# Scaling the shared-key heads behind their values product, and interleaving the long input's first passes with the short projection

## The chip, the cores and the metric

The kernel runs on one core of one Trainium2 chip. A core has five engines with instruction queues of their own: TensorE (PE in the profile; its weight loads are listed as PEld), VectorE (DVE), ScalarE (ACT), GpSimd (POOL) and SyncE (SP), which here issues every DMA. Each queue is worked off in order; an instruction that waits holds up all that stand behind it on its engine. The metric is the device time of one execution in microseconds.

## The reference

The program is one layer of an encoder, applied with shared weights to a long input (1024 tokens) and a short one (512 tokens), each with 16 learned tokens in front. Model width is 1024.

```python
n = rms_norm(h, g_mix)
qa, ka, va, qb, kb, vb = split(n @ w_in)          # 18 blocks of 128 columns
# group A: 8 query heads of 64 columns, 2 key/value heads, each shared by 4 query heads
qa, ka = rope(rms_norm(qa)), rope(rms_norm(ka))
oa = softmax(qa @ ka.T / 8) @ va
# group B: 4 heads, each the difference of two softmax maps
qb, kb = rope(qb), rope(kb)
ob = (softmax(q0 @ k0.T / 8) - lam * softmax(q1 @ k1.T / 8)) @ vb
ob = rms_norm(ob, g_subln) * (1 - lam_init)
h = h + concat(oa, ob) @ w_out
n = rms_norm(h, g_ffn)
h = h + (gelu(conv3(n @ w_gate)) * (n @ w_up)) @ w_down
return rms_norm(h, g_final)[:, 16:]
```

All inputs and outputs are float32. The change touches the front of this: the norm of the input, the order of the projection `n @ w_in`, and the softmax of group A.

## The kernel before

**Products.** A float32 product is made of three fast ones: both operands are split into a rounded part (`hi`) and the rest (`lo`), and `mm3` (L121 to L123) adds hi·hi, hi·lo and lo·hi in PSUM. A split (`split`, L114 and L115) is a copy on ACT and a subtraction on DVE, or on POOL where the caller says so. `load_weight` loads a weight block of [128, 1024] and splits it; where `g.splits` is a list, it notes the two instructions there. `dense` is one output tile: 8 blocks of the contraction, 24 matmuls. Products with `ones_d`, `ones_hd`, `ones_v` (to sum squares over partitions) and the transposes are plain float32 matmuls, which the profile lists as two records each.

**Projection** (`projection`, once per input s; s = 0 is the long input with 1040 columns in chunks of 384, 384 and 272; s = 1 the short one with 528 in chunks of 256 and 272). Columns are tokens. First come eight passes, one per 128 rows of the input: load x, scale and round it on ACT (L234, `xhi`), subtract on DVE (L235, `xlo`), square on ACT (L238). The squares of the short input are summed at once by TensorE into two PSUM tiles (L241); those of the long input are added up on POOL (L245, `acc`), and three matmuls sum them over partitions at the end (L255). `rsqrt_newton` makes `rstd` from the sums, chunk by chunk. Then come 18 weight blocks: K and V of group A, then the four Q blocks of A alternating with the V blocks of B, then K and Q of B in turn. `qk_a` multiplies a product by `rstd` (L312), squares it, sums it (L318), norms and rotates it (`rotary`); `values` multiplies (L333) and transposes (L339). The blocks of B need no norm of their own, so their rope tables are multiplied by `rstd` beforehand on POOL (L366). Results go to DRAM (`g.qk`, `g.v`, `g.vt`).

**Attention** (`attention`). For group A, a block is 512 queries of one head: eight blocks for the short input, sixteen for the long one. For each 128 queries `softmax` makes the scores (L431, L432), DVE moves them out of PSUM with a running maximum (L433), ACT takes the exponential in place and sums it (L438, `l`), DVE takes 1/l (L442) and multiplies the whole tile of [128, keys] by it (L508). When four tiles stand, `weighted_v` transposes them on TensorE in pieces of 128 keys (L456), splits each piece (ACT and DVE), and multiplies by the values (L470, L471), queries along the columns. `finish_a` adds the two halves of the result (ACT L487, DVE L489) into `o_a`, which is stored to `g.oT`. Group B has its own scaling (L532) and is not touched.

**Order.** Each function is a generator that yields the matmul columns it has issued, and `merge` interleaves two of them by weights. The short projection is written alone, to its end. Then the short attention is merged with the long projection, then the long attention with the short input's output projection and feed-forward layer, then the rest of the long input follows. What is written is only the preference: a planner simulates the machine while it lays out the program and gives each engine the first instruction, in the order of writing, that it takes to be ready. `tc.issue_after` (`behind` here) ties an instruction behind another on the same engine's queue; it is an order, not a wait for its end. Before the change, ACT's and DVE's passes of the long input are tied behind the short input's norm (`g.norm_of_short`), and the long input's first product behind the short projection's fourteenth (`g.short_products`). All DMAs go through SP.

## Time and profile before

| | |
|---|---|
| Time before, median of 3 runs | 2134.44 us (2131.06 to 2139.33) |
| The profiled execution | 2127.9 us, of which the span shown by the trace is 2126.1 us |
| TensorE busy in the span | 2040.4 us (96%) |
| VectorE busy | 1725.0 us (81%) |
| ScalarE busy | 1156.0 us (54%) |
| GpSimd busy | 560.8 us (26%) |
| DMA | 296.31 MB, mean 139 GB/s |

The table's busy times are sums over stages with different limits. The lines of a group in the profile give: source line, engine, operation, tiles written and read, shape and count, then the busy time, the mean time of one in ns, and the idle time of that engine just before them with what ended it. A line of waits names the engine and line that waited, what it waited for, the total in us, how often, and the longest. A row of a stretch gives, for each engine, its busy time and number of instructions, then the granted share of TensorE's clock and the DMA share. The chain of waits goes back from the last instruction of a stretch to what released it, step by step; its shares tell which engine the time depended on.

### The profile page before, as it was taken

To read this page: it belongs to the slowest core of one execution; us is meant where nothing else is said; L and a number is where in the kernel's file an instruction comes from. 1 tells how busy PE (TensorE), PEld (TensorE's weight loads), DVE (VectorE), ACT (ScalarE), POOL (GpSimd) and SP (SyncE) were. 2 spreads that over 40 slices of the span, in tenths; PEclk is the share of its full clock that TensorE was granted. 3 is DMA by queue.
4 is the path that set the end of the run, shared out by engine and by line. 5 is a ranking of instruction groups with operands and counts; after the bars stand their busy time and mean duration, and the time that the engine had idled before them with its cause. 6 is when DMAs were issued, how large, how long until landed. Compare 5 with 4: busy or idle time off the path is not lost.

```text
span 2126.1 us, 35236 instructions
## 1 busy us (share of the span) xinstructions
PE 2040.4 (96%) x12302; PEld 1822.3 (86%) x12302; DVE 1725.0 (81%) x3786; ACT 1156.0 (54%) x2253; POOL 560.8 (26%) x494
## 2 busy tenths in 40 slices
PE   6999999998999999999999999988999999999998
PEld 6988888997887989999989999987887777778877
DVE  6878889767879788888998885578778878879886
ACT  6635566544567556666666765345444444435454
POOL 4653233453112000000000000421544444330112
PEclk9999999999999999999999999999999999999999
DMA  7563435457621322223352225996322232247443
GB/s 255 176 203 130 119 111 171 153 178 236 209 79 56 105 75 67 74 82 118 104 187 88 86 97 147 276 290 217 107 100 90 101 113 84 94 167 260 119 126 127
DMA packets 171426, 296.31 MB, mean 139 GB/s; under 512 B 21456, under 2 KB 90608, under 8 KB 170736
## 3 DMA queue, kind: packets, MB, share of 16 engines
q1 hardware_dynamic: 171248, 294.05, 42.5%
q8 instruction: 97, 1.59, 0.3%
q14 instruction: 81, 0.66, 0.1%
HBM read 211.13 MB, written 82.85 MB: 138 GB/s over the span
## 4 chain that ended last, share of the span: by engine, by line
PE 76%; DVE 12%; DMA 4%; issue 3%; ACT 2%; POOL 1%; SPq 0%; DVEq 0%; ACTq 0%; POOLq 0%
PE ps_mm L121 17%; PE ps_mm L123 17%; PE ps_mm L122 17%; PE ps_t L456 5%; PE ps_s L431 3%; PE ps_s L432 3%; PE ps_s L122 2%; PE ps_s L123 2%; PE ps_s L121 2%; DVE p L433 2%; PE ps_o L471 2%; DVE w_lo L115 1%; PE ps_o L470 1%; DVE acc L972 1%; DMA m<-oT 1%
## 5 line engine op out<-in xcount | busy, mean ns | idle before, releaser
L121 PE MATMUL ps_mm<-xhi,w_hi 128*128 128x258 f32 (+3 forms) x1264 | 383.1, 303 | 12.3 <-ACT xhi L114 5.6
L122 PE MATMUL ps_mm<-xlo,w_hi 128*128 128x258 f32 (+3 forms) x1264 | 378.4, 300 | 0.3 <-POOL xlo L115 0.3
L123 PE MATMUL ps_mm<-xhi,w_lo 128*128 128x258 f32 (+3 forms) x1264 | 377.1, 299 | 0.3 <-DVE w_lo L115 0.3
L433 DVE TENSOR_SCALAR_CACHE_REDUCE p<-ps_s 114x344 f32<-114x344 f32 (+4 forms) x562 | 257.8, 489 | 28.1 <-PE ps_s L432 16.8
L114 ACT CAST pt_hi<-ps_t 128x512 fp32r<-128x512 f32 (+6 forms) x360 | 169.6, 484 | 180.8 <-PE ps_t L456 153.3
L121 PEld LDWEIGHTS ps_mm<-xhi,w_hi 128*128 128x128 f32 x1264 | 239.6, 190 | 18.3 <-ACT xhi L114 7.8
L438 ACT ACTIVATE p<-p,nm 114x1040 f32<-114x1040 f32 (+5 forms) x212 | 214.8, 1013 | 70.5 <-DVE nm L436 69.3
L115 DVE TENSOR_TENSOR w_lo<-w_f,w_hi 128x1024 fp32r<-128x1024 f32 (+1 forms) x182 | 195.2, 1080 | 67.3 <-ACT w_hi L114 66.8
L122 PEld LDWEIGHTS ps_mm<-xlo,w_hi 128*128 128x128 f32 x1264 | 240.0, 190 | 1.9 <-POOL xlo L115 0.8
L123 PEld LDWEIGHTS ps_mm<-xhi,w_lo 128*128 128x128 f32 x1264 | 239.4, 190 | 1.2 <-DVE w_lo L115 0.5
L114 ACT CAST w_hi<-w_f 128x1024 fp32r<-128x1024 f32 (+1 forms) x199 | 167.4, 856 | 79.3 <-PE ps_mm L122 52.2
L115 DVE TENSOR_TENSOR pt_lo<-ps_t,pt_hi 128x512 fp32r<-128x512 f32 (+4 forms) x312 | 172.0, 562 | 42.5 <-ACT pt_hi L114 40.9
L115 POOL TENSOR_TENSOR a_lo<-gate,a_hi 128x256 fp32r<-128x256 f32 x44 | 43.1, 981 | 540.9 <-ACT a_hi L114 521.0
L431 PE MATMUL ps_s<-k,q 128*114 128x348 f32 (+4 forms) x552 | 182.7, 336 | 3.2 <-DVE p L433 3.0
L456 PE MATMUL ps_t<-ident,p 128*128 128x128 f32 (+7 forms) x1188 | 182.4, 269 | 0.9 <-DVE nm L436 0.5
L121 PE MATMUL ps_s<-xhi,w_hi 128*128 128x256 f32 (+4 forms) x480 | 148.2, 311 | 23.2 <-DVE t L333 7.7
L432 PE MATMUL ps_s<-k,q 128*114 128x348 f32 (+4 forms) x552 | 170.3, 313 | 0.0
L456 PEld LDWEIGHTS ps_t<-ident,p 128*128 128x128 f32 (+7 forms) x1188 | 139.9, 135 | 29.1 <-issue 6.8
L123 PE MATMUL ps_s<-xhi,w_lo 128*128 128x256 f32 (+4 forms) x480 | 147.0, 307 | 3.2 <-DMA w_lo<-wo 3.0
L122 PE MATMUL ps_s<-xlo,w_hi 128*128 128x256 f32 (+4 forms) x480 | 148.7, 311 | 1.2 <-DVE xlo L115 0.5
L122 PE MATMUL ps_mm<-t_lo,w_hi 128*128 128x512 f32 (+2 forms) x368 | 142.8, 388 | 1.4 <-DVE t_lo L115 1.4
L121 PE MATMUL ps_mm<-t_hi,w_hi 128*128 128x512 f32 (+2 forms) x368 | 142.8, 388 | 0.0
(273 smaller groups left out, 5269.7 us busy)
## 6 DMA issues: line engine op xcount, KB each, us to landing
w_f<-w_gate SPq DMA_DIRECT2D x46, 512.0 KB, 3.4
w_f<-w_up SPq DMA_DIRECT2D x44, 512.0 KB, 3.3
w_f<-w_in SPq DMA_DIRECT2D x36, 512.0 KB, 4.0
a_f<-act SPq DMA_DIRECT2D x62, 256.0 KB, 2.7
w_f<-w_down SPq DMA_DIRECT2D x22, 512.0 KB, 3.4
act<-a_t SPq DMA_DIRECT2D x44, 256.0 KB, 2.1
a<-w_down SPq DMA_DIRECT2D x40, 256.0 KB, 5.4
w_hi<-wo SPq DMA_DIRECT2D x36, 256.0 KB, 5.2
```

Source lines behind the costliest of these rows:

```text
L114: return (nc.scalar.copy(hi, src).ins, (lo_engine or nc.vector).tensor_tensor(out=lo, in0=src, in1=hi.bitcast(F32), op=ALU.subtract).ins)
L115: (lo_engine or nc.vector).tensor_tensor(out=lo, in0=src, in1=hi.bitcast(F32), op=ALU.subtract).ins)
L121: nc.tensor.matmul(ps, lhsT=whi, rhs=xhi, start=start, stop=False)
L122: nc.tensor.matmul(ps, lhsT=whi, rhs=xlo, start=False, stop=False)
L123: return nc.tensor.matmul(ps, lhsT=wlo, rhs=xhi, start=False, stop=stop).ins
L431: nc.tensor.matmul(ps, lhsT=q[0], rhs=k[:, c0:c0 + cw], start=True, stop=False)
L432: nc.tensor.matmul(ps, lhsT=q[1], rhs=k[:, c0:c0 + cw], start=False, stop=True)
L433: nc.vector.tensor_scalar(out=p[:, c0:c0 + cw], in0=ps, scalar1=HD ** -0.5, scalar2=-3.0e38, op0=ALU.mult, op1=ALU.max, accum_out=mx[:, i: ...
L438: g.last_exp = nc.scalar.activation(p, p, AF.Exp, bias=nm, accum_out=l).ins
L456: nc.tensor.transpose(tps[:, c:c + M], p[:, k0:k0 + kw], g.ident[:M, :M])
L470: nc.tensor.matmul(o, lhsT=v[:, i, :], rhs=hi, start=i == 0, stop=False)
L471: nc.tensor.matmul(o, lhsT=v[:, i, :], rhs=lo, start=False, stop=False)
```

## The change

**The softmax of group A.** `softmax` is asked for no inverse; the four sums of a block go to the columns of one tile `l4` [128, 4]. After the fourth, one reciprocal on DVE inverts all four, a DMA stores them as a row of 512 floats in DRAM, and a second DMA reads the row back, broadcast to 64 partitions of a tile `rows`. Blocks alternate between the upper and the lower half of `rows`, and `finish_a` writes `o_a` on the same half. POOL then multiplies `o_a` [64, 512] by `rows` before the store. The multiplication of each [128, keys] tile by 1/l (L508) is gone; the 16 first queries ("halo") keep theirs.

**The long input's passes.** The long input's squares are summed like the short one's: by TensorE, three matmuls for each of the eight passes, into the two "mm" tiles and the "o" tile of PSUM. The long projection's front becomes a generator and is written between the short projection's tiles: after the first five, one pass per two tiles, then `rstd`, two tiles, the first weight and product, and then the rest of the short projection. Each pass is tied behind the last weight split written before it (ACT and DVE), its matmuls behind the last product. The long x has three buffers in place of two.

**Smaller edits.** The first weight of the long projection is loaded late; the long values weight is split behind one of the last short weights; the multiplication of the rope tables is tied behind the fifth rotation; `g.last_rows`, behind which the short output projection's first splits are tied, now names the row maximum in place of L508.

```diff
-    products = []
+    products = g.short_products if s == 1 else []
...
-        if s == 1:
-            ms = [g.psum.tile(P, cw, tag2) for _, cw in chunks]
-        else:
-            acc = sp.tile([P, n], F32, name="acc", bufs=1)
+        ms = [g.psum.tile(P, cw, t) for t, (_, cw) in zip((tag2, tag2) if s == 1 else ("mm", "mm", "o"), chunks)]
         for k in range(KT):
-            x = sp.tile([P, n], F32, name="x", tag="x", bufs=2 if s == 0 else 8)
+            x = sp.tile([P, n], F32, name="x", tag="x", bufs=3 if s == 0 else 8)
...
-                for ins in g.norm_of_short:
-                    order.enter_context(tc.issue_after(ins))
+            with behind(g, *(g.splits[-1] if s == 0 else [])):
...
-                sq = acc if k == 0 and s == 0 else x
-                nc.scalar.activation(sq, x, AF.Square)
-            if s == 1:
+                nc.scalar.activation(x, x, AF.Square)
+            with behind(g, *g.short_products[-1:]):
                 for ps, (c0, cw) in zip(ms, chunks):
                     nc.tensor.matmul(ps, lhsT=g.ones_d, rhs=x[:, c0:c0 + cw], start=k == 0, stop=k == KT - 1)
-            elif k:
-                for c0, cw in chunks:
-                    a = acc[:, c0:c0 + cw]
-                    nc.gpsimd.tensor_tensor(out=a, in0=a, in1=x[:, c0:c0 + cw], op=ALU.add)
+            if s == 0:
+                yield 0
...
+        if s == 0:
+            yield 0
+            with behind(g, *g.splits[-1]):
+                first = load_weight(g, wp, g.w_in[KA], ahead=1)
+            c0, cw = chunks[0]
+            first_ps = g.psum.tile(P, cw, tag)
+            with behind(g, *g.short_products[-1:]):
+                products.append(dense(g, first_ps, first, xhi, xlo, c0, cw))
+            yield 0
...
-        w = load_weight(g, wp, g.w_in[j], ahead=1 + s, lo_engine=nc.gpsimd if s == 0 else None)
+        with behind(g, *(short_splits if j == VA else [])):
+            w = load_weight(g, wp, g.w_in[j], ahead=1 + s, lo_engine=nc.gpsimd if s == 0 else None)
...
-    for tb in tab:
-        nc.gpsimd.tensor_tensor(out=tb, in0=tb, in1=rstd, op=ALU.mult)
+    with behind(g, rotated[4]):
+        for tb in tab:
+            nc.gpsimd.tensor_tensor(out=tb, in0=tb, in1=rstd, op=ALU.mult)
...
-    def finish_a(o, W):
-        low = op.tile([P, 512], F32, name="o_low", tag="w1", bufs=1)[:HD, :W]
-        nc.scalar.copy(low, o[HD:P, :])
+    def finish_a(o, W, half=slice(0, HD)):
+        other = slice(HD - half.start, P - half.start)
+        low = op.tile([P, 512], F32, name="o_low", tag="w1", bufs=1)[half, :W]
+        nc.scalar.copy(low, o[other])
...
+    rows = op.tile([P, 512], F32, name="r_rows", tag="r_rows", bufs=1)
...
+                l4 = sp.tile([P, 4], F32, name="l4", tag="l4", bufs=2)
                 for t in range(4):
-                    p, _, r = softmax([x[:, off + t * P:off + (t + 1) * P] for x in q], k)
-                    g.last_rows = [g.last_exp, nc.vector.tensor_scalar(
-                        out=p, in0=p, scalar1=r, scalar2=None, op0=ALU.mult).ins]
+                    p = softmax([x[:, off + t * P:off + (t + 1) * P] for x in q], k, False, l4[:, t:t + 1])[0]
                     pl.append(p)
+                    if t == 3:
+                        nc.vector.reciprocal(out=l4, in_=l4)
+                        row = g.r[s][h * nblk + b]
+                        nc.sync.dma_start(out=row.rearrange("(t p) -> p t", p=P), in_=l4)
+                        c = (h * nblk + b) % 2 * HD
+                        half = slice(c, c + HD)
+                        nc.sync.dma_start(out=rows[half], in_=row.unsqueeze(0).broadcast_to([HD, 512]))
                     yield 2 * n
                 o, W = yield from weighted_v(pl, v, False)
-                oa = finish_a(o, W)
+                oa = finish_a(o, W, half)
+                nc.gpsimd.tensor_tensor(out=oa, in0=oa, in1=rows[half], op=ALU.mult)
...
-    with ExitStack() as es:
-        drain(projection(es, g, 1, "right", "s", "t"))
-    g.splits = None
     with ExitStack() as es0:
         p0 = projection(es0, g, 0, "left", "mm", "mm")
+        with ExitStack() as es:
+            p1 = projection(es, g, 1, "right", "s", "t")
+            advance(p1, 5)
+            for _ in range(KT):
+                advance(p0, 1)
+                advance(p1, 2)
+            advance(p0, 1)
+            advance(p1, 2)
+            advance(p0, 1)
+            drain(p1)
+        g.short_splits, g.splits = g.splits, None
```

`advance(gen, n)` takes n steps of a generator.

More of the change, by code (lines that the diff above doesn't have):

```diff
@@ L296, in follow @@
                 pending.pop()()
+    short_splits = [] if s == 1 else g.short_splits[-3]
     tab = load_tables(0)
@@ L435, in softmax @@
         nm = sp.tile([P, 1], F32, name="nm", tag="nm")[:M]
-        nc.vector.tensor_reduce(out=nm, in_=mx[:, :nch], axis=AX.X, op=ALU.max, negate=True)
-        l = sp.tile([P, 1], F32, name="l", tag="l")[:M]
-        g.last_exp = nc.scalar.activation(p, p, AF.Exp, bias=nm, accum_out=l).ins
+        most = nc.vector.tensor_reduce(out=nm, in_=mx[:, :nch], axis=AX.X, op=ALU.max, negate=True)
+        if l is None:
+            l = sp.tile([P, 1], F32, name="l", tag="l")[:M]
+        g.last_rows = [nc.scalar.activation(p, p, AF.Exp, bias=nm, accum_out=l).ins, most.ins]
         r = None
@@ L561, in attention @@
         v = load_v(1 + h, 2 * P, 0)
-        rows = g.oT[s][512 + h * P:512 + (h + 1) * P]
+        out = g.oT[s][512 + h * P:512 + (h + 1) * P]
         for blk in blocks:
@@ L569, in attention @@
             c1 = c0 + lead - (NMETA - 1)
-            nc.sync.dma_start(out=rows[:, c1:c1 + W - lead], in_=ob[:, lead:])
+            nc.sync.dma_start(out=out[:, c1:c1 + W - lead], in_=ob[:, lead:])
     if s == 1:
@@ L1229, in merge, with advance @@
             b = None
+def advance(gen, n):
+    for _ in range(n):
+        next(gen)
 def drain(gen):
@@ L1268, in trunk_kernel @@
         g.oT.append(dram.tile([D, N + 1], F32, name=f"oT{s}"))
+        g.r.append([dram.tile([512], F32, name=f"r{s}_{i}") for i in range(8 * N // 512)])
     g.h = dram.tile([KT, P, SEQS[0]], F32, name="h0")
```

37 lines of the change are left out of this document (15 added, 22 removed).

## The prediction

> **What bounds the kernel now.** I began with the page's first lines and then cut the span into stages.
>
> ```profile
> span 2126.1 us, 35236 instructions
> PE 2040.4 (96%) x12302; PEld 1822.3 (86%) x12302; DVE 1725.0 (81%) x3786; ACT 1156.0 (54%) x2253; POOL 560.8 (26%) x494
> ...
> q1 hardware_dynamic: 171248, 294.05, 42.5%
> ```
>
> PE is busy for 96% of the span, so a change to DVE can pay only where PE really waits. The busy times by stretch show where that is. Up to 150 us is the short input's projection; group A's heads (the shared-key heads) of the short input run from 160 to 300, those of the long input from 500 to about 900.
>
> ```profile
> core 0: us, PE busy (x) PEld busy (x) DVE busy (x) ACT busy (x) POOL busy (x), PEclk, DMA share, GB/s
> 26.00:80.00 54.00, 42.49 (x309) 41.28 (x308) 46.48 (x59) 35.55 (x58) 46.84 (x37) 0.91 0.55 181
> 80.00:150.00 70.00, 70.00 (x562) 69.24 (x561) 55.30 (x101) 27.52 (x59) 38.33 (x47) 1.00 0.58 187
> 150.00:160.00 10.00, 5.35 (x20) 4.22 (x19) 5.08 (x9) 4.12 (x9) 2.62 (x5) 0.71 0.76 230
> 160.00:330.00 170.00, 162.70 (x1007) 145.95 (x1006) 145.35 (x455) 101.25 (x234) 54.91 (x55) 0.98 0.41 124
> 500.00:700.00 200.00, 186.43 (x1235) 161.53 (x1234) 172.64 (x508) 126.22 (x230) 36.28 (x49) 0.99 0.44 141
> 700.00:910.00 210.00, 210.00 (x1393) 189.13 (x1393) 172.14 (x441) 121.40 (x200) 15.17 (x17) 1.00 0.25 76
> ```
>
> PE stands idle 11.5 us in 26 to 80, 4.7 us in 150 to 160, 7.3 us in 160 to 330 and 13.6 us in 500 to 700, and not at all in 80 to 150 and 700 to 910. Because a busy PE may still be held up inside its pipeline, I take the chain of waits, stretch by stretch, as the judge of which engine sets the end. In this order: 160 to 330, 500 to 560, 560 to 620, 620 to 680, 680 to 910, 26 to 80.
>
> ```profile
> by line: PE ps_mm L121 11.8%; PE ps_mm L122 11.5%; PE ps_mm L123 11.4%; PE ps_t L456 9.0%; DVE p L433 5.3%; PE ps_o L471 4.4%; PE ps_s L431 3.6%; DVE w L273 3.5%; PE ps_o L470 3.4%; PE ps_s L432 3.3%; ACT p L438 3.3%; DMA qk<-hi 2.9%; issue
> by line: DMA m<-oT 24.3%; DVE p L433 16.9%; DMA q<-qk 9.0%; PE ps_mm L121 4.6%; PE ps_t L456 4.6%; issue 4.4%; PE ps_mm L122 4.4%; PE ps_mm L123 4.2%; DVE w_lo L115 3.8%; DVE xlo L115 3.3%; PE ps_s L431 3.2%; ACT xhi L114 2.6%; PE ps_o L471
> by line: PE ps_mm L122 19.2%; PE ps_mm L121 18.9%; PE ps_mm L123 18.9%; PE ps_t L456 14.3%; PE ps_o L471 6.6%; PE ps_s L432 6.6%; PE ps_o L470 6.6%; PE ps_s L431 6.4%; ACT w_hi L114 1.8%; PE ps_o L480 1.4%; issue 0.0%
> by line: DVE p L433 20.9%; DVE pt_lo L115 13.1%; DVE p L508 7.2%; DVE t L761 7.1%; issue 4.9%; PE ps_mm L121 4.7%; PE ps_mm L122 4.5%; PE ps_t L456 4.1%; PE ps_mm L123 4.0%; DVE pt_hi L115 3.4%; POOL xlo L115 2.9%; ACT pt_hi L114 2.8%; PE p
> by line: PE ps_mm L121 18.6%; PE ps_mm L122 18.5%; PE ps_mm L123 18.3%; PE ps_t L456 15.2%; PE ps_o L471 7.1%; PE ps_o L470 7.0%; PE ps_s L431 7.0%; PE ps_s L432 6.8%; PE ps_o L480 1.6%
> by line: POOL acc L245 16.0%; issue 13.3%; POOL rope L366 7.7%; DMA x<-xT 6.5%; DVE xlo L235 5.9%; POOL w_lo L115 4.4%; DVE hn L107 3.9%; DMA qk<-u 3.6%; DVE w_lo L115 3.3%; DVE w L273 2.5%; DVE w L274 2.4%; DVE t L312 2.2%; ACT xhi L234 2.
> ```
>
> From 560 to 620 and from 680 to 910 the chain is PE alone. From 620 to 680 it is mostly DVE, with the scaling L508 itself on it; 500 to 560 is shared by DMA and DVE; in 160 to 330 PE has 58% of it. In 26 to 80 PE's matmuls are not even among the lines shown: the long input's passes (L245, L235) and the rope tables (L366) are.
>
> **The change, part 1: the scaling of the heads.** These DVE groups go or shrink: first the short stage (160 to 330), then the long one (500 to 910), then how many L508 fall in the two stretches where DVE is on the chain (500 to 560, 620 to 680).
>
> ```profile
> L508 DVE TENSOR_SCALAR p<-p,r 128x528 f32<-128x528 f32 x32 | 20.7, 648 | 0.4
> L442 DVE RECIPROCAL r<-l 128x1 f32<-128x1 f32 (+3 forms) x39 | 6.0, 155 | 4.1 <-ACT p L438 3.8
> L508 DVE TENSOR_SCALAR p<-p,r 128x1040 f32<-128x1040 f32 x64 | 49.5, 775 | 0.4
> L442 DVE RECIPROCAL r<-l 128x1 f32<-128x1 f32 x64 | 10.0, 157 | 8.5 <-ACT p L438 8.2
> 500.00:560.00 60.00, 10.28 (x13) 0.97 0.71 232
> 620.00:680.00 60.00, 8.48 (x11) 1.00 0.21 60
> ```
>
> Short: 20.7 for the 32 scalings, 24 reciprocals fewer (one over [128,4] for four) x 0.155 = 3.7, and some three quarters of the 4.1 waited: about 27.5 us of DVE. The chain is not PE for 42% of that stage, so I take 0.42 x 27.5 = 11.6 us; bounds 0 (PE sets it all) and 27.5. Long: a tile takes 0.775 + 0.157 = 0.93 us of DVE. The 24 tiles in the two DVE stretches are worth 12.1 and 10.3 us; I take 35% of the first (the DMA m<-oT has most of that chain) and 75% of the second, 4.2 + 7.7 = 11.9; bounds 0 and 22.4. The other 40 tiles, 37 us of DVE, lie under a chain that is PE alone: 0. Their cover is PE's saturation; it falls only if PE gets less to do there, and it doesn't.
>
> What is added: 24 multiplies of [64,512] on POOL, and per block of 512 queries two DMAs on SP, a store of 512 single floats and a read-back broadcast to 64 partitions. The nearest rows:
>
> ```profile
> L1017 POOL TENSOR_TENSOR a_t<-act,a_t 128x512 f32<-128x512 f32 x22 | 32.1, 1461 | 1.2 <-DMA act<-a_t 0.3
> oT<-o_a SPq DMA_DIRECT2D x4, 0.2 KB, 3.9
> q<-qk SPq DMA_DIRECT2D x14, 256.0 KB, 3.5
> SPq L175 <- DVE w_lo L115: 150.7, 22, 15.0
> ```
>
> 24 x 1.46 = 35 us of POOL, of which 16 blocks, 23 us, fall on a POOL busy 51 us of 410. It delays only the store of o_a, which the output projection reads after all heads: 0. The store: a row of 64 single floats lands in 3.9 us. For eight times as many the bounds are 3.9 and, if the time grew with the count, 31 us. By the page's queue row a packet takes 42.5% x 16 x 2126 / 171248 = 84 ns of one of the 16 engines, so 512 take 2.7 us: I take 3.9 + 2.7 = 6.6 us, plus 3.5 for the read-back and 1.5 for the multiply, 12 us behind the fourth exponential. A long block lasts 410 / 16 = 26 us, most of which its values product fills, so the rows are there in time. SP is in order: behind the read-back, which waits for the store, stand the loads of queries and weights. SP already stood 150.7 us in 22 weight loads until buffers came free, so a block of 6.6 us has room: 0; bounds 0 and rival 3's price.
>
> Two rows for the multiply's other effect: the same weight split while POOL is busy (10 to 160) and while it hardly works (910 to 1290).
>
> ```profile
> L115 DVE TENSOR_TENSOR w_lo<-w_f,w_hi 128x1024 fp32r<-128x1024 f32 x18 | 26.2, 1454 | 13.0 <-ACT w_hi L114 13.0
> L115 DVE TENSOR_TENSOR w_lo<-w_f,w_hi 128x1024 fp32r<-128x1024 f32 x38 | 46.8, 1239 | 5.1 <-ACT w_hi L114 4.9
> ```
>
> A DVE pass with both inputs in SBUF is 0.2 us slower beside POOL. With 24 multiplies each meeting one or two such passes that is 5 to 10 us of DVE, a fifth of it on the chain: +1.5 us. The Trainium skill (SBUF — State Buffer, "Who interferes with whom") says that such a pass and a GpSimd instruction that reads SBUF exclude each other for the whole instruction. By that rule the charge would be up to a whole multiply per block, 35 us of DVE and some 7 on the chain; the rows, with their mean of 0.2, show the mild form.
>
> **Part 2: the short projection and the long input's passes.** PE's waits from 20 to 160, and the instructions around the longest of them:
>
> ```profile
> PE ps_s L121 <- DVE t L333: 7.7, 2, 6.6
> PE ps_s L121 <- DVE t L312: 2.5, 1, 2.5
> PE ps_mm L255 <- DVE rstd L106: 2.5, 1, 2.5
> PE ps_mm L121 <- DVE rstd L106: 2.1, 1, 2.1
> PE ps_t L318 <- DVE v L115: 1.3, 1, 1.3
> ...
> 43.34 1.16 ACT L234 ACTIVATE xhi<-x,vec 128x1040 fp32r<-128x1040 f32 x1 [3.60 <-DMA x<-xT]
> 44.54 1.30 DVE L235 SCALAR_TENSOR_TENSOR xlo<-x,vec,xhi 128x1040 fp32r<-128x1040 f32 x1 [2.23 <-ACT xhi L234]
> 45.76 0.43 DVE L333 TENSOR_TENSOR t<-ps_s,rstd 128x272 f32<-128x272 f32 x1
> ```
>
> The 6.6 us wait is a long pass in the way: ACT sat 3.6 us on the DMA of a long x, DVE sat 2.2 us on ACT, and t (L333), which empties the short PSUM tile, was queued behind both. The change ties each long pass behind a later short weight split, so it can't stand there: 7.7 + 1.3 = 9.0 us back. The 2.5 us on L312 is the short rstd's own chain and stays. The two waits on rstd (2.5 + 2.1) come from the long rstd being made chunk by chunk, at the end of the short projection; in the change it is done before: 4.6 us back. After them PE ran cold, as the chain in order of time shows (start, duration, instruction; the first rows are of the fp32 sums of squares, for the sum below):
>
> ```profile
> 15.22 2.67 PE ps_t L241 x12
> ...
> 150.63 0.66 PE ps_mm L255 x2
> ...
> 157.43 0.32 PE ps_mm L122
> ...
> 161.41 0.18 PE ps_mm L123
> ```
>
> From 156.7 to 161.2 the 14 matmuls stand 0.32 apart instead of 0.18, another 2 us, so 15.6 back in all; bounds 0 and 23 (with the 2.5 and the clock of 0.91 in 26 to 80, 54 x 0.09 = 4.9). Against it stand the sums of squares: 24 matmuls in place of 3. A fp32 matmul is two records; 384 columns take 0.66 and some 264 take 2 x 2.67 / 12 = 0.45. Eight rows of 384 + 384 + 272 columns are 8 x 1.77 = 14.2, less 1.8 removed: 12.4 us. PE is full from 80 to 150, so I charge it all; bounds 0 (inside idle time that is left) and 12.4 plus a wait of 3.6 on x at each of 8 steps, since they stand in PE's queue ahead of the next product: 41. Net: -3.2 us. Taken at nothing, each with its cover: POOL's additions and rope tables, which leave the front of this stage (what they delayed is in the 9.0; POOL then has 38.3 of 70 us busy to hide the tables in); SP's eight loads of x and the first long weight, issued later but still some 50 us ahead of the long projection's start at 157; the first long product, 24 matmuls that PE does later instead of before 90; the long values weight and the first rows of the output projection, which are only tied to other neighbours. If the loads came late, one step of PE would wait 3.6 us, which the bound of 41 holds.
>
> **Sum.** -11.6 - 11.9 + 1.5 - 3.2 = -25.2 us. The profiled execution took 2127.9 us (span 2126.1 and 1.8 around it), below the three timed runs, whose median is 2134.44. Against it: 2102.7; on the median's footing 2109.
>
> **The rivals.** (1) *DVE's relief does not reach PE.* PE is 96% busy and the chain is PE's own in two of the long stretches; were it so in all, only part 2 would be left: 2134.4 - 3.2 = 2131, no change. Against it: L508 stands on the chain in 620 to 680. (2) *More comes through*: DVE was 85% busy in 160 to 330 and 86% in 500 to 700, and a queue that full delays everything in it. With the upper bounds, 27.5 + 22.4 + 15.6 and the squares in idle time: 2069; half way to it, 2089. (3) *Slower: the read-back blocks SP.* Place: SP's queue in group A. If the store takes far over 6.6 us, SP stands on the read-back while weights are due. From about 22 us on (26 a block less some 4 for its issues) SP sets the block; at 24 us, 16 x (24 + 4) = 448 in place of 410: +38, about 2170. For it: the store is 512 separate floats, a form no row shows. Against it: 84 ns a packet. (4) *The squares aren't paid back*: stalls merely move, +12.4 with part 1 as forecast: 2125.
>
> **How the numbers follow.** Forecast 0.50, own range 2095 to 2123; rival 1 0.14; rival 2 0.18; rival 3 0.09; rival 4 0.09. What a measurement here can tell from no change is 0.5%, about 10.7 us: faster means under 2123.8, slower over 2145.1. Faster: nearly all of the forecast (0.48), rival 2 (0.18) and half of rival 4 (0.05), 0.71. Slower: rival 3 and a little of rivals 1 and 4, 0.11. Same: 0.18. For 8 in 10 the range runs from 2069, rival 2's bound, to 2140, above rival 1.
>
> **What would show it.** In the changed profile L508 is gone; from 620 to 680 DVE leaves the chain and PE's idle time in 500 to 700 is about half of 13.6 us; 680 to 910 is no shorter. PE has no wait of 6 us on t before 80 and none on rstd at 150, and 48 more records of squares, 14 us, stand before 150. The store of the 512 floats lands in 4 to 10 us. It is wrong if SP's wait for that store is followed by ACT waiting for w_f, if PE waits on x's squares, or if 680 to 910 shrinks too.

## The result, and the profile after

The changed kernel is slower: 2183.41 us (median of 4, 2176.48 to 2187.69) against 2133.93 us for the kernel before (median of 4, 2131.06 to 2139.33). The ratio is 1.0235, with a 95% interval of 1.0210 to 1.0260, some 50 us. I had forecast 2109 and a range of 2069 to 2140; the result lies outside it, on the other side.

The first lines of the page of the changed kernel:

```profile
span 2180.4 us, 35335 instructions
...
PE 2069.4 (95%) x12344; PEld 1850.2 (85%) x12344; DVE 1676.2 (77%) x3618; ACT 1154.4 (53%) x2254; POOL 562.8 (26%) x497
```

DVE lost 48.8 us of work, as the change meant it to (1725.0 before). PE got 29 us more busy time, some 15 of it the added sums of squares, and the rest of the longer span is PE standing idle. Busy times by stretch, first of the kernel before, then of the changed one (columns: us, then busy time and instructions of PE, PEld, DVE, ACT and POOL, the granted clock, the DMA share and GB/s):

```profile
160.00:300.00 140.00, 133.16 (x828) 120.14 (x828) 117.72 (x360) 79.02 (x179) 44.52 (x47) 0.97 0.41 127
300.00:400.00 100.00, 95.18 (x620) 88.03 (x619) 86.59 (x292) 64.02 (x167) 36.20 (x26) 0.98 0.48 147
500.00:560.00 60.00, 52.04 (x311) 42.77 (x310) 53.92 (x177) 37.04 (x70) 6.49 (x11) 0.97 0.71 232
560.00:700.00 140.00, 134.39 (x927) 118.76 (x926) 118.72 (x332) 89.18 (x161) 29.79 (x38) 1.00 0.33 102
```

```profile
160.00:300.00 140.00, 117.59 (x708) 105.56 (x707) 93.70 (x281) 70.79 (x162) 46.28 (x52) 0.93 0.41 115
300.00:400.00 100.00, 88.72 (x559) 81.27 (x557) 82.94 (x252) 59.52 (x150) 31.98 (x25) 0.97 0.48 140
500.00:560.00 60.00, 51.31 (x310) 46.89 (x309) 36.81 (x114) 26.86 (x54) 17.55 (x22) 0.94 0.57 189
560.00:700.00 140.00, 124.08 (x815) 110.00 (x813) 94.97 (x269) 78.55 (x148) 26.83 (x33) 0.94 0.49 128
```

In the four stretches PE is busy 33 us less, 15.6 of it in the short input's shared-key heads (160 to 300) and 10.3 between 560 and 700, where the short input's output projection stands. By start times in the trace, the short attention's last square sums begin 26 us later than before (523.4 against 497.2), and the last sum of the short output projection and its residual (h) begins 53 us later (673.1 against 619.8). The traced executions differ by 54 us, so nearly the whole loss is there by 673.

What SP waited for between 150 and 650, in the changed kernel (engine and line, releaser, us in total, times, longest):

```profile
SPq L517 <- DMA r<-l: 100.7, 12, 10.6
SPq L275 <- ACT hi L114: 42.9, 22, 3.8
```

The read-back (L517) has become SP's largest wait by far. SP's own timeline shows one such wait, in the second short block:

```profile
189.52 0.39 SPq L514 DMA_DIRECT2D r<-l  x1
198.78 0.48 SPq L517 DMA_DIRECT2D r_rows<-r  x1
199.35 1.19 SPq L398 DMA_DIRECT2D q<-qk  x2
200.63 0.54 SPq L175 DMA_DIRECT2D w_f<-w_in  x1
```

The store of 512 floats is issued at 189.52, and SP issues nothing until 198.78. Directly behind stand the next block's queries (L398) and the next weight (L175). The answer of the store's line on how long a transfer takes from issue to landing:

```profile
DMA to landing us min/median/max: 7.5/9.1/13.4
```

I had taken 6.6 us. The chain of waits from 500 to 620 shows the same thing at the start of the short output projection:

```profile
by line: DMA m<-oT 23.6%; DVE p L429 8.4%; PE ps_mm L121 7.8%; DMA res<-xT 7.8%; PE ps_mm L122 7.4%; PE ps_mm L123 7.3%; PE ps_t L453 3.6%; issue 2.7%; DVE pt_lo L115 2.1%; ACT p L435 1.6%; ACT xhi L114 1.6%; PE ps_o L468 1.5%; PE ps_o L467
...
541.67 9.11 DMA m<-oT
551.20 4.00 DMA m<-oT
559.94 12.92 DMA m<-oT
...
587.69 9.35 DMA res<-xT
```

The attended rows m that open the projection, and the residual rows, hold the chain in pieces of 4 to 13 us. In the kernel before, the chain of the same stretch has no residual rows, and three pieces of m, 14.6 us together; the longest two:

```profile
526.05 7.00 DMA m<-oT
533.97 4.48 DMA m<-oT
```

That much the trace of the changed kernel says by itself. It doesn't say how much of the 50 us is SP standing, how much the slow store does to other transfers, and what became of DVE's relief.

### The profile page after: what moved, and what is told of

The parts are those of the page before. It is cut to its first block, busy times and chain, and to the rows that moved or that the text cites. A ratio compares the mean times of both kernels' runs of the same rounds, so it can differ in the third digit from the quotient of the medians.

```text
span 2180.4 us, 35335 instructions
## 1 busy us (share of the span) xinstructions
PE 2069.4 (95%) x12344; PEld 1850.2 (85%) x12344; DVE 1676.2 (77%) x3618; ACT 1154.4 (53%) x2254; POOL 562.8 (26%) x497
## 2 busy tenths in 40 slices
DMA packets 186018, 299.50 MB, mean 137 GB/s; under 512 B 34512, under 2 KB 103664, under 8 KB 185328
## 4 chain that ended last, share of the span: by engine, by line
PE 56%; DVE 8%; DMA 6%; ACT 2%; issue 2%; SPq 0%; POOL 0%; DVEq 0%; ACTq 0%; POOLq 0%
PE ps_mm L123 14%; PE ps_mm L121 14%; PE ps_mm L122 13%; PE ps_t L453 4%; PE ps_s L427 2%; PE ps_s L428 2%; DMA m<-oT 2%; DVE w_lo L115 1%; DMA w_lo<-wo 1%; DVE acc L980 1%; PE ps_o L468 1%; PE ps_o L467 1%; DVE p L429 1%; DMA res<-xT 1%; PE ps_s L123 1%
## 5 line engine op out<-in xcount | busy, mean ns | idle before, releaser
L429 DVE TENSOR_SCALAR_CACHE_REDUCE p<-ps_s 114x344 f32<-114x344 f32 (+4 forms) x562 | 258.4, 489 | 51.4 <-PE ps_s L428 34.1
L453 PE MATMUL ps_t<-ident,p 128*128 128x128 f32 (+7 forms) x1188 | 187.6, 272 | 0.6 <-DVE nm L432 0.5
```

The source lines that it names most:

```text
L429: nc.vector.tensor_scalar(out=p[:, c0:c0 + cw], in0=ps, scalar1=HD ** -0.5, scalar2=-3.0e38, op0=ALU.mult, op1=ALU.max, accum_out=mx[:, i: ...
L453: nc.tensor.transpose(tps[:, c:c + M], p[:, k0:k0 + kw], g.ident[:M, :M])
```

## The experiments

Each kernel was timed beside runs of the kernel before on the same chip, whose medians lay between 2130.25 and 2133.02 us. 0.001 of the ratio is 2.1 us.

| kernel | time, us | ratio to the kernel before, 95% interval |
|---|---|---|
| e1 passes only | 2133.49 | 1.0015 (1.0002 to 1.0028) |
| e2 scaling only | 2166.26 | 1.0163 (1.0139 to 1.0187) |
| e3 read-back without its wait | 2151.69 | 1.0097 (1.0068 to 1.0126) |
| e4 rows by TensorE | 2147.93 | 1.0077 (1.0055 to 1.0099) |
| e5 no scaling | 2130.46 | 0.9996 (0.9976 to 1.0015) |
| e6 store only | 2145.59 | 1.0087 (1.0059 to 1.0116) |
| e7 read-back written later | 2178.90 | 1.0227 (1.0194 to 1.0259) |
| e8 store of 128 x 16 B | 2136.82 | 1.0022 (1.0004 to 1.0040) |
| e9 turned store, read-back written later | 2139.92 | 1.0047 (1.0029 to 1.0064) |
| e10 read-back tied behind the values | 2173.13 | 1.0202 (1.0173 to 1.0231) |
| e11 long heads only | 2151.98 | 1.0099 (1.0075 to 1.0123) |
| e12 before, scaled twice | 2165.81 | 1.0156 (1.0123 to 1.0189) |
| e13 128 x 16 B, rows in order | 2138.21 | 1.0030 (1.0014 to 1.0046) |
| e14 the same, old passes | 2131.71 | 0.9996 (0.9979 to 1.0013) |
| e15 store of 512 x 16 B | 2139.60 | 1.0029 (1.0011 to 1.0048) |
| e16 store of 128 x 4 B | 2164.52 | 1.0151 (1.0118 to 1.0183) |
| e17 read-back issued by POOL | 2204.48 | 1.0336 (1.0310 to 1.0362) |
| e18 store of 512 x 4 B, 64 B apart | 2134.35 | 1.0010 (0.9996 to 1.0024) |

### Which part: e1 and e2

e1 is the changed kernel with the attention of the kernel before; e2 is the changed attention on the projection of the kernel before.

> The projection and its order as in the change, the attention as before (every tile scaled by L508, no row of inverse sums). Theory S (SP stands behind the read-back, which waits 9.5 us for the store of the 512 floats; what is late are the loads behind it): the passes are harmless, 2125 to 2140 us. Rival P (the passes and their sums of squares on TensorE cost the time): 2170 us or more.

> The attention as in the change, the projection and its order as before. Theory S: the whole loss stays, 2170 to 2190 us. Rival P: the loss is gone and the relief of DVE is left, 2105 to 2125 us.

Part 2 alone makes hardly a difference (+3 us, interval 0 to 6), and part 1 alone carries +35, most of the loss, though not the whole of it that theory S expected. Together they lose 50, so part 2 costs 15 us more in company with part 1 than the +3 it costs alone would suggest; e13 and e14 come back to that.

### The wait, and rows without DMA: e3 and e4

```diff
e3
-  nc.sync.dma_start(out=rows[half], in_=row.unsqueeze(0).broadcast_to([HD, 512]))
+  nc.sync.dma_start(out=rows[half], in_=g.rope_in[0][0, 0:512].unsqueeze(0).broadcast_to([HD, 512]))
e4
-  (the store and the read-back)
+  r4 = [op.tile([P, P], F32, name="r4", tag="e", bufs=6) for _ in range(2)]
+  for i2, rt in enumerate(r4):
+      nc.gpsimd.tensor_copy(rt.rearrange("p (t c) -> p t c", t=2),
+                            l4[:, 2 * i2:2 * i2 + 2, None].broadcast_to([P, 2, HD]))
...
+  for t in range(4):
+      nc.tensor.matmul(rps[:, t * P:(t + 1) * P], lhsT=r4[t // 2][:, t % 2 * HD:(t % 2 + 1) * HD],
+                       rhs=g.ident, start=True, stop=True)
+  nc.scalar.copy(rows[:HD], rps)
```

> The changed kernel, but the second DMA reads a fixed row of the rope tables in place of the row just stored, so it waits for no store; both DMAs, the multiply and all else stay (group A's heads are scaled by numbers that are not the inverse sums). Theory S: SP does not stand, the loss of 49 us goes and the relief of DVE shows, 2095 to 2120 us. Rival P, or a rival that the number of small DMA packets or the multiply costs the time: 2170 us or more.

> The changed kernel without the two DMAs: POOL spreads the four inverse sums over 64 columns each, four plain float32 matmuls against the identity make the row on 64 partitions in PSUM, ACT copies it out and POOL multiplies as in the change. It adds 24 x 4 matmuls of 128 columns, some 0.22 us each, 21 us of TensorE, and 24 copies on ACT. Theory S: faster than the change by 40 us or more, 2100 to 2135 us. Rival P: 2180 us or more.

Both missed what I expected, on the same side. Without the wait 29 of the 50 us go (1.0235 to 1.0097), and 21 stay. In e3 no instruction of SP waits for the store in the read-back, yet the transfers of the short output projection land late. The rows of the kernel before, then of e3, from 150 to 620 (median us from issue to landing at the end of the row):

```profile
w_f<-w_out SPq DMA_DIRECT2D x8, 512.0 KB, 5.2
m<-oT SPq DMA_DIRECT2D x8, 129.0 KB, 3.4
...
m<-oT SPq DMA_DIRECT2D x8, 127.5 KB, 3.8
```

```profile
w_f<-w_out SPq DMA_DIRECT2D x8, 512.0 KB, 8.2
m<-oT SPq DMA_DIRECT2D x8, 129.0 KB, 6.1
...
m<-oT SPq DMA_DIRECT2D x8, 127.5 KB, 6.3
```

So a second cost beside the wait came into sight: these transfers land some 3 us later, although the read-back waits for no store. e3 still has the read-back's own traffic; e6 below does without it. e4 has neither DMA, has the relief of DVE, and gives PE 96 fp32 matmuls more (four for each of 24 blocks), which I had put at 21 us; it takes 16 us more than the kernel before. With a relief of 23.5 us it would have been no slower, which was the first sign that the relief is worth little.

### What the relief is worth: e5 and e12

e5 drops the reciprocal of the four sums, the store, the read-back and the multiply. e12 is the kernel before with L508 done twice.

> The changed kernel with the reciprocal of the four sums, the store, the read-back and the POOL multiply all left out: the shared-key heads stay unscaled, so their numbers are wrong, and only the relief of DVE and the rewritten projection remain. My forecast's sum without its +1.5 for the multiply and with part 2 at the +1.4 that the passes alone measured: 2132.5 - 23.5 + 1.4 = 2110. If DVE's relief does not reach PE (rival 1): 2130 to 2136. If the changed attention loses time by something other than the two DMAs (the order of the rows that the short output projection is tied to): above 2140.

> The kernel before with every scaling of a shared-key head done twice (so the numbers are wrong): 20.7 + 49.5 = 70 us of DVE more, the mirror of what the change takes away. If DVE has room in these stages, as taking the scalings out (no change) suggests: within 10 us of the kernel before. If DVE's time is on the path by the shares my forecast used (42% of 20.7, 35% and 75% of the long tiles in two stretches): +18 to +25, 2150 to 2157; and far more, up to +70, if DVE has no room at all where it is full and only less work, not more, is hidden.

With all of DVE's relief, none of its price, and part 2 as written, e5 takes the time of the kernel before (0.9996). It bears part 2's cost as well: against e1, part 2 alone, the relief is worth some 4 us, with about 5 either way, in place of the 23.5 that I forecast. A kernel with the relief alone was not run. e12 shows that DVE is not idle either: 70 us of DVE work more cost 33 us, more than the mirror of my shares (18 to 25). Taking work from DVE gives little, adding it costs nearly half of it. The stretches show why. This is e5, for the same four stretches as above:

```profile
160.00:300.00 140.00, 133.50 (x831) 120.49 (x830) 108.73 (x321) 83.62 (x187) 44.39 (x49) 0.98 0.43 135
300.00:400.00 100.00, 89.12 (x557) 83.72 (x556) 89.47 (x255) 55.80 (x146) 34.14 (x25) 0.91 0.45 141
500.00:560.00 60.00, 52.37 (x300) 44.78 (x299) 44.55 (x150) 35.97 (x70) 6.74 (x12) 0.91 0.73 244
560.00:700.00 140.00, 137.93 (x970) 123.95 (x969) 107.05 (x293) 92.40 (x168) 27.02 (x38) 1.00 0.34 106
```

DVE is busy 9.0 us less in 160 to 300, and PE does no more there (133.50 against 133.16). In 500 to 560 DVE is busy 9.4 us less, and PE again the same. Only from 560 to 700 does PE get 3.5 us more done. From 300 to 400, where next to nothing was taken from DVE (the short input's other heads), PE does 6.1 us less than before.

### The price of the store: e6

The changed kernel with the store, without read-back and multiply.

> As the kernel with no scaling, but with the reciprocals and the stores of 512 single floats kept; no read-back, no multiply. What it takes above the kernel with no scaling is the price of the store on the transfers issued behind it. If the stores cost by their own slowness: 10 to 20 us above the kernel with no scaling (the read-back without a wait left 19 over the kernel before). If only the wait of SP on the read-back costs: within 4 us of it.

At 1.0087 it stands 19 us above e5 by the ratios, 15 by the medians, with some 7 either way. Nothing reads this store's data; the chain of waits at the short output projection shows where it costs. From 500 to 620 m<-oT and the residual rows hold 36 us of that chain in e6; in e5 no piece of m is among its 200 longest, and the residual rows hold 4.3 us. The longest two pieces in e6:

```profile
516.27 12.31 DMA m<-oT
533.44 10.57 DMA m<-oT
```

The DMA queue shows that the stores slow what runs beside them. From 160 to 300 the packets of e6, then of e18, which stores as many single floats 64 B apart (packets, MB, share of the time of 16 DMA engines):

```profile
q1 hardware_dynamic: 15693, 18.47, 64.8%
```

```profile
q1 hardware_dynamic: 16418, 18.63, 44.2%
```

For the same bytes the DMA engines are taken up half as long again; in e5, without stores, the share is 42.1%. From e6 to the changed kernel it is another 32 us, the read-back's wait and the multiply. So 50 = 0 (relief and part 2) + 19 (the store) + 32 (SP behind it), within the intervals. This is a ladder of kernels, not two separate sums inside the changed one: there SP's standing itself keeps transfers from going out behind the store, and m lands in 2.9 and 3.5 us (medians).

### Attempts to move the wait: e7, e10 and e17

```diff
e7    (the read-back written behind the values product; e10: inside "with behind(g, values_done[-1])")
                 o, W = yield from weighted_v(pl, v, False)
                 oa = finish_a(o, W, half)
+                nc.sync.dma_start(out=rows[half], in_=row.unsqueeze(0).broadcast_to([HD, 512]))
                 nc.gpsimd.tensor_tensor(out=oa, in0=oa, in1=rows[half], op=ALU.mult)
e17   (at the place of the changed kernel)
-                        nc.sync.dma_start(out=rows[half], ...
+                        nc.gpsimd.dma_start(out=rows[half], ...
```

> The changed kernel with the read-back issued behind the values product, where the multiply stands, instead of right behind the store. SP then reaches it when the store has long landed. If the 32 us of the read-back's wait are SP standing on it, they come back: 2150 to 2156, and the milestones of the short attention return to those of the kernel whose read-back waits for nothing (its end 508 instead of 523). If the read-back's wait costs in another way (the multiply late, o_a late): still over 2165.

> The changed kernel with the read-back tied behind the last matmul of its block's values product. In the run before this one the read-back was only written later, and the kernel's order of work still put it a few instructions behind the store: SP stood on it for 103.8 us as before. Here it is really late. If the 32 us are SP standing on the store's landing: the wait on r goes, and it takes 2148 to 2156, like the read-back that waits for nothing (2152). If the loads behind the slow store are what is late anyway: still over 2165.

> The changed kernel with the read-back issued by POOL, so that POOL stands on the store of 512 floats and SP does not. Two attempts to move the read-back later in SP's queue left it in place. If SP standing there is the 32 us: 2150 to 2158, as with the read-back that waits for nothing, and the SP wait on r is gone. If POOL standing 24 times some 8 us delays its weight splits by as much: over 2170.

The waits of e7, of e10 (SP, 150 to 650) and of e17 (POOL, the same window):

```profile
SPq L520 <- DMA r<-l: 103.8, 12, 11.8
```

```profile
SPq L521 <- DMA r<-l: 103.9, 12, 10.4
```

```profile
POOL r_rows L517 <- DMA r<-l: 108.0, 10, 15.8
```

e7 and e10 failed as experiments. Few transfers lie between a block's store and its read-back in SP's order, so the read-back stayed at nearly the same place in the queue, and SP stood on it as long as before. They show only that the same queue gives nearly the same time. e17 does move the wait, and POOL is the worse place for it: POOL stands 108 us, SP waits 34.1 us in 9 weight loads for POOL's splits (15.5 us in 7 in the changed kernel), and the kernel takes 72 us more than the kernel before. Its read-backs also go over another queue (software_dynamic in the profile), so the place of the wait is not all that differs. What a read-back far behind its store on SP would cost was not tried.

### Why the store is slow: e8, e9, e15, e16 and e18

```diff
changed  out=row.rearrange("(t p) -> p t", p=P), in_=l4              512 pieces of 4 B, side by side
e8       out=row.rearrange("(p t) -> p t", p=P), in_=l4              128 pieces of 16 B, side by side
e9       TensorE transpose of l4, ACT copy, then
         out=row.rearrange("(t p) -> t p", p=P), in_=lt              4 pieces of 512 B
e15      out=row.rearrange("(t p x) -> p t x", p=P, x=4), in_=wide   512 pieces of 16 B, side by side
e16      out=row[0:P].unsqueeze(1), in_=l4[:, 0:1]                   128 pieces of 4 B, side by side
e18      out=row.rearrange("(t p x) -> x p t", p=P, x=16)[0], in_=l4 512 pieces of 4 B, 64 B apart
```

> The changed kernel with the store written as 128 runs of 16 B (each partition's four sums side by side) in place of 512 single floats; the rows come out in another order, so the heads are scaled by wrong numbers. If the store's landing grows with its pieces: between the 3.9 us of 64 pieces and the 9.1 of 512, some 4.5 us, so SP stands 12 x 4 us less on it and the kernel comes to 2145 to 2155. If a store read back costs 9 us whatever its pieces: 2175 to 2185.

> The read-back late as in the run beside it, and the four reciprocals turned by TensorE and copied by ScalarE, so that the store writes 4 rows of 512 B instead of 512 single floats (24 transposes of 128 x 128 more on PE, some 5 us). If the number of single pieces is what makes the stores costly, it is 10 to 20 us below the run with the late read-back, 2135 to 2142, and the store lands in 3 to 4 us; if any store and read-back on SP cost the same, it is no faster than that run.

> The changed kernel storing 512 pieces of 16 B (each sum four times side by side, made by a small POOL copy); the read-back takes the first 512 floats of it, so the heads are scaled by wrong numbers. If the number of pieces sets the landing: 9 us as with 512 of 4 B, and a time of 2170 to 2190. If pieces of 4 B are what is slow: some 3 to 4 us, as with 128 of 16 B, and 2137 to 2150.

> The changed kernel storing only the first of each partition's four sums, 128 pieces of 4 B side by side in memory, and reading back those 128; only a quarter of the queries are scaled, by the wrong sums. If a piece of 4 B costs by itself (512 of them land in 9.1 us, 512 of 16 B in 3.1): about a quarter of the 6 us more, a landing of some 3 to 4.5 us, and 2135 to 2150.

> The changed kernel storing its 512 floats 64 B apart in memory in place of side by side; the read-back takes one float for 64 partitions, so it still waits for the store but moves almost nothing, and the heads stay unscaled but for one query. If single floats are slow because of their size: landing 9 us again, and 2165 to 2185. If they are slow because neighbouring floats share a stretch of memory: 3 to 4 us and 2130 to 2145.

How long these stores take to land, in this order: e8, e15, e16, e18 (the changed kernel's 9.1 stands above):

```profile
DMA to landing us min/median/max: 1.4/2.8/6.4
```

```profile
DMA to landing us min/median/max: 2.4/3.1/5.8
```

```profile
DMA to landing us min/median/max: 6.2/8.0/11.1
```

```profile
DMA to landing us min/median/max: 1.8/2.6/6.6
```

The traces of e6 and e9 tell no landing. The changed kernel and e15 move the same number of pieces: the pages of both count 186018 packets, that of e18 186019.

The number of pieces is not it: 512 pieces land in 3.1 us (e15). The size of a piece alone is not it either: 512 pieces of 4 B, each 64 B from the next, land in 2.6 us (e18). Slow are single floats written side by side, and there the count matters little: 128 of them take 8.0 us (e16), 512 take 9.1. My expectation for e16, a quarter of the extra time, was wrong, and e8, at 2137, lies below both times that I had named for it. e9, with 4 pieces of 512 B, comes to 1.0047; its read-back is written late as in e7 (1.0227). The time of the kernel goes with the landing: 2.6 to 3.1 us go with ratios of 1.0010 to 1.0029, 8.0 and 9.1 us with 1.0151 and 1.0235. (e16 and e18 also read back less, 128 floats and one to each partition; e8 and e15 read back as much as the changed kernel.) Why neighbours are slow (whether it is the stretch of memory that they share, and how large it is) stays open: between 4 B and 16 B side by side, and between 4 B and 64 B of distance, nothing was measured.

### The place, and a cheap store: e11, e13 and e14

e11 uses the new scaling in the long input's heads alone. e13 and e14 store 128 pieces of 16 B, and the multiply puts the rows back in order:

```diff
-  nc.gpsimd.tensor_tensor(out=oa, in0=oa, in1=rows[half], op=ALU.mult)
+  o4 = oa.rearrange("c (t p) -> c t p", p=P)
+  nc.gpsimd.tensor_tensor(out=o4, in0=o4, in1=rows[half].rearrange("c (p t) -> c t p", p=P), op=ALU.mult)
```

> The changed kernel with the new scaling in the long input's heads alone; the short input's heads are scaled as before. If, as the milestones say, 26 of the 50 us arise in the short heads and the rest at the start of the short output projection: 2150 to 2160. If all of it comes from the long stage, as my rival placed it: 2175 to 2185. If the short stage alone carries it: 2130 to 2137.

> The changed kernel with the store as 128 runs of 16 B, and the POOL multiply reading the rows with a step of four elements, so that every query meets its own sum. If the step costs POOL nothing that counts: the 2137 of the run with 128 runs, 0 to 0.4% over the kernel before. If the relief of DVE were worth what my forecast said (23 us), it would now show: under 2115; the kernel with no scaling at all took 2130, so I expect 2130 to 2142.

> The same store and multiply, with the short projection and the long input's passes of the kernel before: only the scaling is changed. If part 2 is neutral, as its run alone showed (ratio 1.0015), the same as the run beside it within 6 us, 2130 to 2142. If part 2 costs 17 us in company with the new scaling, as the two kernels with the 512 floats differ by: 2115 to 2125, and then it would beat the kernel before.

e11, which has part 2 as well, loses 21 us, so the long heads and part 2 carry some two fifths of the loss, and the new scaling of the short heads brings the other 29 us. e13, the whole change with another layout of its store, is 6 us slower than the kernel before, not 50: 43 us hang on how 2 KB are laid out. e14, the scaling alone with that store, is level with the kernel before (0.9996). Part 2 costs 7 us between the two, and the store, read-back and multiply 7 us between e5 and e13. Taken as sums, e5, e14 and e13 put the relief at 8 us, with about 6 either way: about a third of the forecast. No version here beats the kernel before beyond its interval.

e14 differs from the kernel before in nothing but the scaling, so its stretches read most cleanly:

```profile
160.00:300.00 140.00, 134.38 (x825) 121.05 (x824) 108.93 (x323) 83.98 (x190) 53.36 (x54) 0.95 0.43 132
300.00:400.00 100.00, 92.26 (x590) 85.81 (x589) 82.83 (x270) 58.66 (x158) 34.70 (x26) 0.95 0.47 146
500.00:560.00 60.00, 52.55 (x306) 44.36 (x305) 43.91 (x150) 33.91 (x66) 11.09 (x13) 0.94 0.65 213
560.00:700.00 140.00, 137.40 (x961) 122.95 (x961) 108.58 (x301) 92.63 (x169) 35.89 (x43) 1.00 0.38 113
```

DVE is busy 32.7 us less in the four stretches, and PE 1.8 us more: +1.2, -2.9, +0.5 and +3.0.

## Why the prediction was wrong, step by step

**The store and the read-back, "0; bounds 0 and rival 3's price".** This is the step that failed first, and it brought the wrong sign: a term put at nothing that cost some 50 us. It had three parts.

- The landing. I scaled by packets: 64 floats land in 3.9 us, and 512 packets at 84 ns of one of 16 engines add 2.7. Both ends of that sum were unfit. The 84 ns are a mean over transfers of all sizes, and the 64 floats of oT<-o_a go to 64 different rows of oT, far apart as in e18. The store measured 9.1 us, between my 6.6 and the 31 that I had as the upper bound.
- The room. "SP already stood 150.7 us in 22 weight loads, so a block of 6.6 us has room" took a sum over the long stage (500 to 910) as slack everywhere. 133.9 us of it lie behind 680; between 150 and 650 these waits are 16.8 us in 3 loads (the row stands below the list), and what stands behind the read-back there is soon needed: the next block's queries, a weight, the rows m. The wait cost some 30 us (e3, and e6 against the changed kernel), at 9 us a store and not from 22 on.
- What I had not priced at all: the slow store makes other transfers late even if nobody waits for it, 19 us (e6 against e5).

The row for the second point, SP in the kernel before from 150 to 650:

```profile
SPq L175 <- DVE w_lo L115: 16.8, 3, 9.2
```

**Rival 3, 0.09.** Its mechanism, SP standing on the read-back while loads are due, is the one that happened. Its place and its point of decision were wrong: I put it into the long stage, where a block lasts 26 us. By e11 more than half of the loss, 29 us, comes with the short blocks (140 us for 8, about 17 us each). Rival 3's 2170 was worked out for a store of 24 us; that the result came near was chance.

**DVE's relief, -11.6 and -11.9.** The second step that failed. Measured: 4 to 8 us by the differences above, each with 5 to 6 either way, and no kernel that has the relief is clearly faster (e5 0.9996, e14 0.9996). DVE's time fell as worked out, but the share of the chain of waits in which DVE stood was taken as the share of the relief that reaches the end. The chain names whoever came last; that the next one is close behind when DVE comes earlier fits these times, but was not followed wait by wait. The rows quoted could have warned: PE's idle time in the stretches concerned was 7.3 + 13.6 = 20.9 us, less than the 23.5 I meant to win. Rival 1 (relief does not reach PE, 2131) was nearly right for this term. In 560 to 700 some relief does come through (+3.0 in e14), and little of it is left at the end. In 680 to 910 the forecast of 0 holds, as does PE's saturation there.

**Part 2, -3.2.** Its waits went as said. All that is left of PE's waits from 20 to 160 in the changed kernel is the short rstd's own chain, which was to stay:

```profile
PE ps_s L121 <- DVE t L309: 2.5, 1, 2.5
```

The squares cost a little more than the 14.2 us (12.4 net) that I charged; the rows of the two column widths, by busy time:

```profile
L236 PE MATMUL ps_mm<-x,ones_d 128*128 128x384 f32 x32 | 11.8, 485 | 0.0
...
L236 PE MATMUL ps_o<-x,ones_d 128*128 128x272 f32 x16 | 5.0, 392 | 0.0
```

That is 16.8 less the 1.8 removed. The stretches up to 200 of the kernel before, then of e1:

```profile
0.00:150.00 150.00, 130.84 (x964) 127.24 (x965) 115.57 (x193) 80.32 (x143) 85.87 (x89) 0.97 0.63 210
150.00:200.00 50.00, 41.36 (x236) 37.08 (x235) 38.51 (x119) 24.69 (x57) 16.09 (x23) 0.86 0.47 151
```

```profile
0.00:150.00 150.00, 140.25 (x1002) 132.94 (x1003) 109.63 (x199) 83.13 (x149) 61.69 (x67) 0.99 0.62 210
150.00:200.00 50.00, 45.85 (x281) 42.32 (x280) 40.02 (x117) 24.13 (x53) 20.11 (x25) 0.93 0.54 174
```

PE's busy time rose by 13.9 us there, idle time won back, against 15.6 forecast; the squares take 15.0. Balance +1 rather than -3.2, and +3 (0 to 6) by e1's ratio. The mechanism was right, the two terms were off by 1.7 and 2.6 us. That part 2 costs 7 us with a cheap store and some 15 with the slow one was not foreseen; which of its steps does that was not tried.

**The multiply, +1.5, and POOL beside DVE.** Here I weighed a rule against two rows and chose the rows. The Trainium skill (SBUF — State Buffer, "Who interferes with whom") says that a DVE instruction with two SBUF inputs and a GpSimd instruction that reads SBUF exclude each other for the whole instruction, and that whoever issues first keeps the port. I read a mean difference of 0.2 us as a mild form. The trace agrees with the rule: the last section has one such meeting, and it costs nearly the whole instruction. A mean over passes of which most meet nothing says little about those that do. What the multiplies cost in all was not measured by itself; in e13 it is at most part of 7 us, the distance from e5.

**The signs I had named.** L508 is gone, the wait on t before 80 and those on rstd at 150 are gone, and 680 to 910 is no shorter; these came true. DVE also left the chain from 620 to 680 (its largest share there is 1.6%), but the store r<-l came in, with 9.2%. ACT's waits for the weights w_f behind the read-back, the sign against me, came weakly (5.9 us from 150 to 910, 2.5 before): late on the chain were m and the residual rows instead. PE's idle time in 500 to 700 was to halve from 13.6 us; it grew to 24.6 (60 - 51.31 + 140 - 124.08), which told against the forecast. The store's landing lay inside "4 to 10 us", so that sign was drawn too wide to warn.

## What to carry to other kernels

Price a small store by a row of the same layout, not the same size: single floats written side by side landed in 8 to 9 us here, and 16 B pieces, or floats 64 B apart, in about 3. Ask of every DMA that waits for another DMA what stands behind it in its queue at that very block; a queue's total of waiting elsewhere is no room. And be wary of a relief priced above the idle time of the engine that bounds the stage (20.9 us here): where two engines are both nearly full, take the chain's share of one of them as an upper bound, and test the other direction too.

## What the runs showed of the hardware that was not expected

**Neighbouring floats.** 512 single floats side by side in device memory: 9.1 us to land; 64 B apart: 2.6 us; as many pieces of 16 B side by side: 3.1 us; 128 floats side by side: 8.0 us (medians of 24 stores).

**A DVE pass beside POOL.** In e5, DVE's p<-p,c (two inputs in SBUF) took 2.90 us; its usual duration at this size is 0.77. DVE's timeline, then POOL's:

```profile
310.63 2.90 DVE L534 SCALAR_TENSOR_TENSOR p<-p,c 102x528 f32<-102x528 f32 x1
```

```profile
310.61 2.36 POOL L115 TENSOR_TENSOR w_lo<-w_f,w_hi 128x1024 fp32r<-128x1024 f32 x1 [1.53 <-ACT w_hi L114]
```

POOL's weight split had begun 0.02 us earlier, and DVE's pass ended 0.56 us after it, somewhat less than the 0.77 that it takes by itself: the two ran all but one after the other. Behind it the last values product waited:

```profile
PE ps_o L477 <- DVE pt_hi L115: 2.8, 1, 2.8
```

The same meeting is in the traces of e13 (313.18, 2.90 us) and of the changed kernel (333.32, 2.90 us); in the kernel before the longest such pass takes 1.31. It stands in 300 to 400, where e5 loses PE time. That it accounts for a part of that loss is likely, but it was not tested by itself. It is hardly large: e1 has two such passes (2.57 and 2.87 us) and takes 3 us more than the kernel before.
